# Splitting a third chunk of the mixer's output product, and issuing gate and spill loads from POOL's queue

## The chip, the cores and the metric

The kernel runs on one core of a Trainium2 chip. TensorE (PE) does the matrix products; VectorE (DVE), ScalarE (ACT) and GpSimd (POOL) do the elementwise work; SyncE (SP) only issues DMA transfers, and ACT and POOL can issue them too. Sixteen DMA engines move the data. The metric is the device time of one execution in microseconds: before the change 3697.25 us, the median of three runs (3697.02 to 3698.64).

## The reference

Two blocks of two layers each on tokens of width 1024. The first block takes 256 tokens `x` and 256 context tokens `ctx`. A layer mixes tokens (differential attention, a pooling branch and a convolution branch, gated and summed) and then applies a PEER network: per token and head the 16 best of 128 x 128 experts are chosen, and their rows of `u` and `v` used.

```python
# mixer, layer l: h is x (256 tokens), hc is ctx (256 tokens)
merged = g[:, :, 0] * attn + g[:, :, 1] * pool + g[:, :, 2] * conv
mix = merged @ w_out                       # 1024 x 1024
h = h + mod[:, 2] * mix                    # ctx alike, with its own mod
xn2 = modulate(rms_norm(h, norm2_g[l]), mod[:, 3], mod[:, 4])
# PEER: eidx and gate come from the top 16 of q @ sub_keys
hid = gelu(einsum('td,thkd->thk', xn2, u_emb[eidx]))
h = h + mod[:, 5] * einsum('thk,thkd->td', gate * hid, v_emb[eidx])
```

The second layer needs `ctx` only for keys and values. The second block (retention and block-sparse attention) is not touched by the change.

## The kernel before, in words

**Products.** Activations lie transposed, with the width on the partitions in eight chunks of 128 and the tokens along the free axis. A product in float32 is made of three matmuls of reduced precision: each operand is split into a high and a low half, and hi·hi, lo·hi and hi·lo are accumulated (lines 393 to 395; one output chunk of 128 takes 8 x 3 matmuls). A weight unit of 1 MB is loaded by SP into a buffer `wraw` (`wload`, line 348, its DMA in line 351). ACT writes the high half (`uhi` or `vhi`, line 361), DVE the low half (`ulo` or `vlo`, line 362). The buffer is free for the next load when DVE has read it. In the values loop these buffers form a ring of three.

**The mixer's output product** (`mixer_out`, line 1022). In layer 0 x and ctx are multiplied by `w_out` together, 512 columns at a time. Chunks below `whole` (line 1061) are done that way; the others are done for x first, then for ctx, 256 columns each. After a chunk, DVE adds it to the residual (`hT`, line 1088), ACT squares it, and POOL and DVE add up the squares (`ssacc`, line 445). When x's chunks are complete, `norm_split` takes the mean of the squares on PE (`ps_ss`, line 464), the inverse root on POOL (`rst`, line 470), spreads it with PE (`ps_y`), and DVE and ACT make the normed halves `xl` and `xh` (lines 491 to 496), while PE does ctx's chunks. Then the same for ctx, and PE can start the PEER queries.

**PEER, layer 0.** 384 of 512 tokens are handled densely: all 16384 experts are evaluated, and a gate tensor with zeros for the experts that weren't chosen is multiplied in. The experts come in 64 blocks of 256. While the gates are being found, the hidden values of the first 42 blocks are computed ahead and written to DRAM (`hd`); the expanded gates are in DRAM too (`gd`). The last 128 ctx tokens are handled by rows: POOL gathers the chosen rows of `u` and then of `v` with 128 + 128 indirect DMAs (class `Rows`, line 258, one row per token and gather, 512 KB). They go into five buffers, and each gather waits for a marked matmul of PE ("beat"), so that they are spread over PE's work. DVE multiplies and sums a `u` row (line 274), PE sums the `v` rows (`ps_row`, line 307).

**The values loop** goes over the 64 blocks. For each, `prep` (line 1199) fetches the gates `G` (line 1556, 768 KB for two blocks, two buffers), gets the hidden values, multiplies both on DVE (line 1213) and splits the result into `Wh` (ACT, line 422) and `Wl` (DVE, line 423). For the 42 blocks computed ahead the hidden values are loaded back (`hs_r`, line 1209, 384 KB, two buffers); for the other 22 they are computed on the spot, in `hidden` with `ps_mm`. Blocks of both kinds alternate in pairs, and the last 20 blocks are all of the first kind. PE then adds the block's product with `v` into PSUM: four accumulators `keep` for 256 tokens, and two `ps_v` that DVE adds to `racc` (line 1236). `values_tok` (line 1269) holds the matmuls. In the same stretch the next layer's modulation weights `wraw_m` are loaded (line 624).

SP's list before holds the loads of weights, `G` and `hs_r` in the order in which the program asks for them, POOL's list the row gathers. The very first `G` is issued by POOL. In layer 1 there are no rows, and `self.rows` is None.

Of the kernel before, what the change touches and what calls it, by code (L numbers as in the profile page):

```python
# [23 lines left out]
KD = 8  # L24
# [305 lines left out]
class Prog:  # L330
# [689 lines left out]
    def mixer_out(self, l, merged, hT, T, right, bulk):  # L1020

        nc, w = self.nc, self.g[f"wa{l}"]
        segs = [(s * 256, (s + 1) * 256) for s in range(T // 256)]
        sts = [self.sumsq(256) for _ in segs]

        def add(c, ps, n, t0, t1):
            self.residual(l, 2, c, hT, ps, t0, t1, old)
            for i, (a, b) in enumerate(segs):
                if t0 <= a and b <= t1:
                    self.sumsq_add(sts[i], hT[:, c, a:b], c)  # L1030
        with ExitStack() as cx:
            mp = cx.enter_context(self.tc.tile_pool(name=f"mp4{l}", bufs=1, reuse_waits="tile"))
            self.pn = cx.enter_context(self.tc.tile_pool(name=f"pn{l}", bufs=1, space=PSUM, reuse_waits="tile"))
            mh = mp.tile([P, KD, T], F32R, tag="mh", name="mh")
            ml = mp.tile([P, KD, T], F32R, tag="ml", name="ml")
            old = hT
            if l == 0:
                old = mp.tile([P, KD, 512], F32, tag="old", name="old")
            k = 0
            for _ in chain([0], bulk):  # L1040
                while k < 6 and k in self.pooled:
                    self.split(mh[:, k], ml[:, k], merged[:, k])
                    k += 1
            ple = None
            if l == DEPTH - 1:
                ple = self.ple(0, lambda tt, h: hT[:, 4 * tt + 2 * h:4 * tt + 2 * h + 2, 0:256], mp)
                next(ple)
            it = self.units(f"wa{l}", 45, 4)
            units = [next(it) for _ in range(3)]
            for k in range(0, KD if l == 0 else 0, 2):  # L1050
                nc.sync.dma_start(old[:, k:k + 2], self.g["hx"][:, k:k + 2])
            first = self.chunks_mm(units, mh, ml, 0, T, range(KPOOL[l]))
            self.pool_out(l, self.last_pool, T, (self.pn, "py", 2))
            self.chunks_mm(units, mh, ml, 0, T, range(KPOOL[l], 6), first, KPOOL[l])
            for k in range(6, KD):
                self.split(mh[:, k], ml[:, k], merged[:, k])
            self.chunks_mm(units, mh, ml, 0, T, range(6, KD), first, 6)
            right.close()
            if l == 0:
                hT = self.resid()  # L1060
            whole = KD if T == 256 else 6
            for c in range(whole):
                add(c, first.pop(0)[:, :T] if first else self.chunk_mm(next(it), mh, ml, 0, T), 0, 0, T)
                if c == 5 and l == DEPTH - 1:
                    self.turn_residual(hT, 0)
            ends = [next(it) for _ in range(whole, KD)]
            xn = None
            for i, (t0, t1) in enumerate(segs):
                for c, unit in zip(range(whole, KD), ends):
                    add(c, self.chunk_mm(unit, mh, ml, t0, t1), i, t0, t1)  # L1070
                if i == 0:
                    self.preload(f"wa{l}", range(49, 51 - l))
                if ple:
                    next(ple)
                xn = self.norm_split(hT, sts[i], lambda k, s: self.mod[:, l, 4, k, s:s + 1],
                                     lambda k, s: self.mod[:, l, 3, k, s:s + 1], [(i, t0, t1)], out=xn, first=t0, mid=ple)
            self.dump(f"h{l}m", hT)
            if l == DEPTH - 1:
                self.turn_residual(hT, 1)
                for _ in ple:  # L1080
                    pass
        return xn, hT
# [117 lines left out]
    def prep(self, l, b, xh, xl, T, gd, hd):  # L1200

        nc = self.nc
        G = self.gates(l, b, gd, T // GSTAGE, T)
        hs = self.hsp.tile([P, 2, T], F32, tag="hs", name="hs_r", bufs=2)
        if b >= NLEAD[l]:
            for _ in self.hidden(l, b, xh, xl, T, hs):
                pass
        else:
            nc.sync.dma_start(hs, hd[b])
        Wh = self.pp.tile([P, 2, T], F32R, tag="Wh", name="Wh", bufs=2)  # L1210
        Wl = self.pp.tile([P, 2, T], F32R, tag="Wl", name="Wl", bufs=2)
        w = hs.rearrange("p j (q t) -> p j q t", t=GSTAGE)
        nc.vector.tensor_tensor(w, w, G.rearrange("p q j t -> p j q t"), op=ALU.mult)  # L1213
        self.split(Wh, Wl, hs)
        return Wh, Wl
# [334 lines left out]
    def gates(self, l, b, gd, nq, T):  # L1550
        nc = self.nc
        key = (l, b // 2)
        if self.gcur is None or self.gcur[0] != key:
            G = self.pp.tile([P, nq, 4, GSTAGE], F32, tag="G", name="G", bufs=2)
            n = nq if self.gcur else nq - 1
            (nc.sync if self.gcur else nc.gpsimd).dma_start(G[:, :n].rearrange("p q j t -> p q (j t)"),
                              gd[:n, :, (b // 2) * 4:(b // 2) * 4 + 4, :].rearrange("q p j t -> p q (j t)"))
            if n < nq:
                nc.gpsimd.tensor_copy(G[:, n], self.glast)
            self.gcur = (key, G)  # L1560
        return self.gcur[1][:, :, (b % 2) * 2:(b % 2) * 2 + 2, :]
# [367 lines left out]
```

## Time and profile before

| | |
|---|---|
| time, median of 3 runs | 3697.25 us (3697.02 to 3698.64) |
| profiled execution | 3701.45 us, span 3699.7 us |
| PE busy | 3574.0 us, 97% of the span |
| DVE, ACT, POOL busy | 67%, 44%, 16% |
| DMA traffic | 777.60 MB, mean 210 GB/s |
| of it queue q1, in hardware | 567.29 MB |
| of it queue q0, in software (POOL's) | 135.41 MB |

Busy time is counted per engine; an engine that isn't busy either waits for another or has nothing to do. A row of waits names the engine that waited, and after the arrow what ended its wait. In the timeline a figure in brackets is the idle time just before the instruction. A DMA's row on SP or POOL is its issue, and not the transfer.

### The profile page before, as it was taken

How to read it: one execution, taken by the hardware profiler on the slowest of the kernel's cores; microseconds unless marked ns; L12 is line 12 of the kernel's file. 1: busy time of each engine (PE TensorE's matmuls, PEld its weight loads, DVE VectorE, ACT ScalarE, POOL GpSimd, SP SyncE). 2: the span in 40 equal slices, each digit the busy share in tenths (PEclk: the TensorE clock that was granted, in tenths of full speed). 3: DMA queues.
4: the chain of work that ended last, by engine and by line, in shares of the span. 5: the costliest groups of instructions: out<-in, count | busy, mean ns of one | idle time of the engine just before them, and what ended most of it. 6: DMA issues, size and time to landing. Idle time of an engine off the chain costs nothing.

```text
span 3699.7 us, 55016 instructions
## 1 busy us (share of the span) xinstructions
PE 3574.0 (97%) x21681; PEld 3097.0 (84%) x21681; DVE 2461.5 (67%) x4540; ACT 1634.3 (44%) x2608; POOL 604.0 (16%) x686
## 2 busy tenths in 40 slices
PE   7999999899999998999999999999999999999999
PEld 5988877789999877776766799999998888887787
DVE  5566556599697777744445677778876555557675
ACT  3334333336576322222222354555676444445454
POOL 0112222100011232322222121221000000002121
PEclk9999999999999999999999999999999999999999
DMA  5222145224689898888889533354578766766453
GB/s 212 75 86 80 69 154 216 75 83 170 228 323 336 315 332 306 325 295 309 298 321 325 188 115 120 120 175 160 200 269 292 244 236 237 242 231 212 145 174 111
DMA packets 227763, 777.60 MB, mean 210 GB/s; under 512 B 17296, under 2 KB 100752, under 8 KB 168496
## 3 DMA queue, kind: packets, MB, share of 16 engines
q1 hardware_dynamic: 165984, 567.29, 43.7%
q0 software_dynamic: 37184, 135.41, 10.4%
q10 hardware_dynamic: 24336, 71.38, 5.0%
q8 instruction: 170, 2.79, 0.3%
q14 instruction: 89, 0.73, 0.1%
HBM read 705.60 MB, written 68.42 MB: 209 GB/s over the span
## 4 chain that ended last, share of the span: by engine, by line
PE 41%; DVE 4%; DMA 2%; ACT 1%; issue 1%; POOL 1%; DVEq 0%; ACTq 0%; SPq 0%; POOLq 0%
PE keep L1269 12%; PE ps_mm L393 5%; PE ps_mm L395 5%; PE ps_mm L394 5%; PE ps_wide L395 2%; PE ps_wide L393 2%; PE ps_wide L394 2%; PE ps_v L1269 1%; DVE ulo L362 1%; PE ps_nar L393 1%; PE ps_nar L395 1%; PE ps_nar L394 1%; DMA wraw<-in_v 1%; PE ps_mm L414 1%; PE ps_row L307 1%
## 5 line engine op out<-in xcount | busy, mean ns | idle before, releaser
L361 ACT ACTIVATE uhi<-wraw 128x1024 fp32r<-128x1024 f32 x586 | 609.0, 1057 | 879.2 <-PE ps_mm L394 336.1
L393 PE MATMUL ps_mm<-xh,uhi 128*128 128x256 f32 (+2 forms) x2952 | 955.5, 324 | 9.2 <-ACT hs L1566 3.7
L395 PE MATMUL ps_mm<-xh,ulo 128*128 128x256 f32 (+2 forms) x2952 | 940.8, 319 | 7.1 <-DVE ulo L362 7.1
L362 DVE TENSOR_TENSOR ulo<-wraw,uhi 128x1024 fp32r<-128x1024 f32 x586 | 718.0, 1237 | 340.6 <-ACT uhi L361 317.6
L394 PE MATMUL ps_mm<-xl,uhi 128*128 128x256 f32 (+2 forms) x2952 | 939.9, 318 | 0.0
L393 PEld LDWEIGHTS ps_mm<-xh,uhi 128*128 128x128 f32 x2952 | 562.5, 191 | 54.0 <-issue 9.2
L395 PEld LDWEIGHTS ps_mm<-xh,ulo 128*128 128x128 f32 x2952 | 562.2, 191 | 29.4 <-DVE ulo L362 8.0
L394 PEld LDWEIGHTS ps_mm<-xl,uhi 128*128 128x128 f32 x2952 | 562.7, 191 | 20.8
L362 DVE TENSOR_TENSOR vlo<-wraw,vhi 128x1024 fp32r<-128x1024 f32 x184 | 224.0, 1222 | 187.7 <-ACT vhi L361 187.5
L361 ACT ACTIVATE vhi<-wraw 128x1024 fp32r<-128x1024 f32 x184 | 193.2, 1056 | 338.1 <-DMA wraw<-in_v 176.0
L1269 PE MATMUL keep<-vlo,Wh 128*128 128x512 f32 x656 | 256.7, 391 | 3.6 <-DVE vlo L362 3.6
L1269 PE MATMUL keep<-vhi,Wh 128*128 128x512 f32 x656 | 257.8, 393 | 0.5 <-ACT Wh L422 0.5
L1269 PE MATMUL keep<-vhi,Wl 128*128 128x512 f32 x656 | 256.2, 391 | 0.3 <-DVE Wl L423 0.3
L258 POOL DMA_INDIRECT row<-in_urow,eu x128 | 158.5, 1238 | 589.7 <-PE ps_mm L395 440.7
L1213 DVE TENSOR_TENSOR hs_r<-hs_r,G 128x768 f32<-128x768 f32 (+1 forms) x128 | 105.2, 823 | 170.7 <-DMA hs_r<-hd 106.9
L393 PE MATMUL ps_nar<-uhi,xh 128*128 128x256 f32 x704 | 201.3, 286 | 2.3 <-ACT cs L664 2.3
L394 PE MATMUL ps_nar<-ulo,xh 128*128 128x256 f32 x704 | 200.1, 284 | 0.0
L395 PE MATMUL ps_nar<-uhi,xl 128*128 128x256 f32 x704 | 199.9, 284 | 0.0
L258 POOL DMA_INDIRECT row<-in_vrow,ev x128 | 136.0, 1063 | 375.4 <-PE keep L1269 180.2
L1530 ACT ACTIVATE stage<-ps_g 128x512 f32<-128x512 f32 x160 | 165.1, 1160 | 1.7 <-DMA wraw<-in_u 0.8
L274 DVE CUSTOM_DVE_ANT_0 row<-row,xt 128x1024 f32<-128x1024 f32 x128 | 155.2, 1219 | 4.5 <-DMA row<-in_urow,eu 4.5
L1269 PEld LDWEIGHTS keep<-vhi,Wh 128*128 128x128 f32 x656 | 123.7, 189 | 36.8 <-issue 9.2
(428 smaller groups left out, 6965.2 us busy)
## 6 DMA issues: line engine op xcount, KB each, us to landing
wraw<-in_u SPq DMA_DIRECT2D x128, 1024.0 KB
wraw<-in_v SPq DMA_DIRECT2D x128, 1024.0 KB
wraw<-in_wa SPq DMA_DIRECT2D x104, 1024.0 KB
wraw<-in_wb SPq DMA_DIRECT2D x50, 1024.0 KB
gd<-stage ACTq DMA_DIRECT2D x80, 512.0 KB
wraw_m<-in_wmod SPq DMA_DIRECT2D x24, 1024.0 KB
G<-gd SPq DMA_DIRECT2D x31, 768.0 KB
mraw<-in_wmod SPq DMA_DIRECT2D x16, 1024.0 KB
```

The lines of the kernel that those rows point to most:

```text
L258: ins = self.nc.gpsimd.indirect_dma_start(row, None, self.p.g[name], bass.IndirectOffsetOnAxis(ap=idx, axis=0))
L274: ins = nc.vector.tensor_tensor_reduce(out=row, in0=row, in1=self.xt, op0=ALU.mult, op1=ALU.add, scale=1.0, scalar=0.0, accum_out=self.hid ...
L307: nc.tensor.matmul(ps[c:c + 32, :], m[:, g, :], rows[n - 4 + g][:, h * 512:(h + 1) * 512], start=(i == 0), stop=(i == 31), tile_position=( ...
L361: nc.scalar.activation(hi, r, AF.Copy)
L362: nc.vector.tensor_tensor(lo, r, hi.bitcast(F32), op=ALU.subtract)
L393: nc.tensor.matmul(ps, lh, rh, start=(i == 0), stop=False)
L394: nc.tensor.matmul(ps, lh, rl, start=False, stop=False)
L395: self.beat = nc.tensor.matmul(ps, ll, rh, start=False, stop=(i == n - 1))
L414: self.nc.tensor.matmul(ps[:, t0:t1], a[:, s], b[:, k, t0:t1], start=(n == 0 and i == 0), stop=(n == KD - 1 and i == 2))
L1213: nc.vector.tensor_tensor(w, w, G.rearrange("p q j t -> p j q t"), op=ALU.mult)
L1269: self.beat = self.nc.tensor.matmul(ps, a[:, j, t], b[:, c], start=(start and j == 0 and i == 0), stop=(stop and j == 1 and i == 2), skip_ ...
L1530: nc.scalar.activation(st[:, :, tb:tb + 4].rearrange("p j t -> p t j"), pg, AF.Copy, scale=1.0 / GSCALE)
```

## The change

In line 1061 `whole` becomes 5 for layer 0, so chunks 5, 6 and 7 of the output product are computed for x and ctx apart; before, these were 6 and 7. In lines 1209 and 1556 the loads of `hs_r` and `G` are issued by POOL instead of SP as long as `self.rows` is set, which is in layer 0.

```diff
@@ mixer_out
-            whole = KD if T == 256 else 6
+            whole = KD if T == 256 else 5
@@ prep
-            nc.sync.dma_start(hs, hd[b])
+            (nc.gpsimd if self.rows else nc.sync).dma_start(hs, hd[b])
@@ gates
-            (nc.sync if self.gcur else nc.gpsimd).dma_start(G[:, :n]...)
+            (nc.sync if self.gcur and not self.rows else nc.gpsimd).dma_start(G[:, :n]...)
```

On POOL, at the start of layer 0's values loop, the row gathers stood in two unbroken runs; the difference shows what stands among them now (`row<-in_urow` is a gather, x9 means nine in a row):

```order
-L258 DMA row<-in_urow,eu 128x1024 x96
-L258 DMA row<-in_vrow,ev 128x1024 x128
+L1556 DMA G<-gd_6364 128x12x128
+L258 DMA row<-in_urow,eu 128x1024 x9
+L1209 DMA hs_r<-hd_6365 128x768
+L258 DMA row<-in_urow,eu 128x1024 x2
+L1556 DMA G<-gd_6364 128x12x128
+L258 DMA row<-in_urow,eu 128x1024
+L1209 DMA hs_r<-hd_6365 128x768
+L258 DMA row<-in_urow,eu 128x1024 x2
+L1556 DMA G<-gd_6364 128x12x128
+L258 DMA row<-in_urow,eu 128x1024 x11
```

Each load now stands between gathers, two loads of each kind for every pair of blocks computed ahead in the first part of the loop.

On SP, in the same place, the loads that stood between weights are gone (`wraw_m` are modulation weights):

```order
 L351 DMA wraw<-in_u 128x2048
-L1209 DMA hs_r<-hd_6340 128x768
-L624 DMA wraw_m<-in_wmod 128x2048
-L1209 DMA hs_r<-hd_6340 128x768
-L1556 DMA G<-gd_6339 128x12x128 x2
-L351 DMA wraw<-in_v 128x2048
-L351 DMA wraw<-in_u 128x2048
-L351 DMA wraw<-in_v 128x2048
-L624 DMA wraw_m<-in_wmod 128x2048
-L351 DMA wraw<-in_v 128x2048 x2
-L1209 DMA hs_r<-hd_6340 128x768
-L351 DMA wraw<-in_u 128x2048
```

The weights follow in the order they had, with nothing between them.

On DVE, in the mixer's output product of layer 0, the residual additions `hT` of ctx stand behind x's norm (`n`, `xl`):

```order
+L362 TENSOR_TENSOR ulo<-wraw,uhi 128x1024
+L496 SCALAR_TENSOR_TENSOR xl<-n_6221,mod,xh 128x256
 L496 SCALAR_TENSOR_TENSOR xl<-n_6225,mod,xh 128x256
 L496 SCALAR_TENSOR_TENSOR xl<-n_6229,mod,xh 128x256
-L496 SCALAR_TENSOR_TENSOR xl<-n_6233,mod,xh 128x256
-L1088 SCALAR_TENSOR_TENSOR hT<-ps_mm,mod,old 128x256 x2
+L1088 SCALAR_TENSOR_TENSOR hT<-ps_mm,mod,old 128x256 x3
 L218 CAST idr<-ident 128x128
 L445 TENSOR_TENSOR ssacc<-ssacc,sq 128x256
 L466 TENSOR_SCALAR rst<-ps_ss 128x2
```

Three additions follow where two did, and three splits of a weight's low half stand among the norm's instructions instead of two.

## Rows read from the trace of the kernel before

**Rows 1.** The page, its first part: busy time, share of the span and instructions of each engine.
```profile
PE 3574.0 (97%) x21681; PEld 3097.0 (84%) x21681; DVE 2461.5 (67%) x4540; ACT 1634.3 (44%) x2608; POOL 604.0 (16%) x686
```
**Rows 2.** Windows of the values loop: length, busy us, then granted clock, DMA share, GB/s.
```profile
1190.00:1600.00 410.00, 380.35 (x1817) 322.60 (x1816) 290.33 (x393) 122.28 (x150) 127.09 (x104) 0.96 0.87 317
1600.00:2100.00 500.00, 490.81 (x2417) 343.14 (x2416) 239.12 (x328) 131.71 (x153) 131.77 (x126) 0.99 0.86 305
```
**Rows 3.** PE's waits from 1190 to 1600 us: total, times, longest.
```profile
PE ps_mm L393 <- DVE racc L1236: 16.1, 6, 4.5
PE ps_mm L393 <- ACT uhi L361: 7.3, 2, 4.2
```
**Rows 4.** Timeline from 1310 us: start, duration, engine, line, instruction.
```profile
1310.56 0.33 SPq L1209 DMA_DIRECT2D hs_r<-hd  x1
1310.93 7.06 SPq L1556 DMA_DIRECT2D G<-gd  x2
...
1317.52 1.22 DVE L362 TENSOR_TENSOR ulo<-wraw,uhi 128x1024 fp32r<-128x1024 f32 x1
...
1318.76 0.35 SPq L351 DMA_DIRECT2D wraw<-in_v  x1
```
**Rows 5.** Timeline from 1328 us, the end of the same chain.
```profile
1328.13 2.00 ACT L361 ACTIVATE uhi<-wraw 128x1024 fp32r<-128x1024 f32 x2 [7.51 <-DMA wraw<-in_v]
...
1332.64 0.68 DVE L1236 TENSOR_TENSOR racc<-racc,ps_v 128x512 f32<-128x512 f32 x1
...
1333.38 0.45 PE L393 MATMUL ps_mm<-xh,vhi 128*128 128x384 f32 x1 [3.91 <-DVE racc L1236]
```
**Rows 6.** Windows of PE's wait and of what follows it, columns as above.
```profile
1329.40:1333.30 3.90, 0.07 (x1) 0.00 (x0) 3.90 (x6) 0.73 (x1) 1.51 (x1) 1.00 1.01 417
1333.30:1336.80 3.50, 3.42 (x14) 3.42 (x15) 1.78 (x5) 1.10 (x2) 0.00 (x0) 0.70 1.03 419
```
**Rows 7.** Windows behind the mixer, columns as above.
```profile
699.70:713.30 13.60, 10.88 (x45) 10.01 (x46) 6.64 (x17) 5.51 (x13) 0.71 (x1) 0.50 0.20 72
713.30:720.00 6.70, 6.70 (x57) 6.70 (x56) 0.00 (x0) 0.00 (x0) 0.00 (x0) 0.98 0.01 2
```
**Rows 8.** Timeline of the mixer's end, 690 to 700 us.
```profile
693.29 1.22 DVE L362 TENSOR_TENSOR ulo<-wraw,uhi 128x1024 fp32r<-128x1024 f32 x1
...
697.19 0.87 DVE L1088 SCALAR_TENSOR_TENSOR hT<-ps_mm,mod,old 128x256 f32<-128x256 f32 x2
...
698.34 0.72 POOL L445 TENSOR_TENSOR ssacc<-ssacc,sq 128x256 f32<-128x256 f32 x1 [10.58 <-ACT sq L434]
...
699.67 0.56 PE L464 MATMUL ps_ss<-mean,ssacc 128*128 128x1 f32 x2 [7.47 <-DVE ssacc L445]
```
**Rows 9.** DMA from 1190 to 2100 us: queue q0, and issues with KB each.
```profile
q0 software_dynamic: 32736, 119.22, 36.8%
...
G<-gd SPq DMA_DIRECT2D x31, 768.0 KB
...
hs_r<-hd SPq DMA_DIRECT2D x42, 384.0 KB
```
**Rows 10.** The tile G: engine, operation, count, ns minimum, median and maximum, first and last.
```profile
L1556 POOL DMA_DIRECT2D G<-gd x2: 1067/1122/1176, 1190.3 to 2828.5; - x2
```
**Rows 11.** Waits of all engines from 1190 to 2100 us.
```profile
POOL row L258 <- PE keep L1269: 227.5, 86, 10.6
...
DVE row L274 <- DMA row<-in_urow,eu: 4.5, 3, 2.4
```
**Rows 12.** Windows with POOL's G in flight, then SP's, columns as above.
```profile
1192.00:1196.00 4.00, 4.00 (x25) 4.00 (x24) 2.26 (x2) 1.44 (x2) 0.00 (x0) 1.00 1.03 418
1201.00:1204.00 3.00, 3.00 (x20) 3.00 (x19) 0.00 (x0) 0.86 (x1) 0.94 (x1) 1.00 1.05 339
```
**Rows 13.** SP's waits from 1190 to 2100 us.
```profile
SPq L1556 <- DVE hs_r L1213: 120.0, 20, 8.9
SPq L1209 <- DVE Wl L423: 112.7, 26, 10.1
```
**Rows 14.** The line of the row gathers, 1190 to 2100 us, columns as for the tile G.
```profile
L258 POOL DMA_INDIRECT row<-in_vrow,ev x128: 934/937/1966, 1586.7 to 2079.5; - x128
```

More of the change, by code (lines that the diff above doesn't have):

```diff
@@ L1555, in gates @@
             n = nq if self.gcur else nq - 1
-            (nc.sync if self.gcur else nc.gpsimd).dma_start(G[:, :n].rearrange("p q j t -> p q (j t)"),
+            (nc.sync if self.gcur and not self.rows else nc.gpsimd).dma_start(G[:, :n].rearrange("p q j t -> p q (j t)"),
                               gd[:n, :, (b // 2) * 4:(b // 2) * 4 + 4, :].rearrange("q p j t -> p q (j t)"))
```

## The prediction

> **What bounds the kernel now.** Of the page I read the engine row first [rows 1]: TensorE (PE) is busy 97% of the span, so only its remaining idle time and its stretches at the low clock can be won. The profiled execution took 3701.45 us (span 3699.7, 1.75 around it), 4.20 above the median of 3697.25; I work out differences in it and take them from the median. Two places are touched: the norm behind the mixer's output product (about 690 to 720 us), and layer 0's values loop (1190 to 2100 us), the only place where `self.rows` is set.
>
> Next come the windows of the values loop [rows 2]. The first 410 us hold 29.65 us without a matmul, the other 500 hold 9.19. The mean granted clock of the first stretch is 0.96. The DMA engines are busy 87 and 86% of the two, so weights, gates and spilled hidden values arrive with little to spare.
>
> PE's own table of waits in the first stretch [rows 3] gives 16.1 us, in six waits, to VectorE's (DVE) `racc` and 7.3, in two, to ScalarE's (ACT) `uhi`: 23.4 of the 29.65. These are links of one chain, which the timeline shows in full [rows 4, 5]. SyncE (SP) issues an hs, two G loads until 1317.99, and at 1318.76 the weight load `wraw<-in_v`. ACT waits for that load until 1328.13, 9.4 us after its issue; DVE splits the low halves behind ACT, a row reduction and the `racc` follow, which frees a PSUM buffer, and PE starts at 1333.38 after 3.91 us idle. The wait put down to DVE is thus a late weight. The windows around it [rows 6] show two more things: while PE waits, the DMA engines run full (share 1.01, 417 GB/s), and behind the wait the granted clock is 0.70, so part of these 3.5 us ran at the lower of the two levels.
>
> **The change part by part.**
>
> *Mixer.* Chunk 5 is computed as two products of 256 columns instead of one of 512: 24 matmuls of 512 columns go, 48 of 256 come. The columns in all are the same, so I leave PE's own time unchanged. A matmul of 256 columns takes 6.70/57 = 0.1175 us [rows 7]. The x half is now followed by three ctx products of 24 x 0.1175 = 2.8 us each instead of two, so x's norm may start 2.8 us earlier against the end. On DVE x's norm ran up to the `hT` pair at 697.19, where the ctx residuals went on, and PE stood idle until 699.67 for the sum of their squares [rows 8]. Of the 2.8 us, one more `ulo` inside the norm takes 1.2, a third `hT` 0.4, a second POOL addition of squares 0.7 (each from its row there [rows 8]). That leaves 2.8 - 1.2 - 0.4 - 0.7 = 0.5 gained. Bounds: if the shorter gap let PE keep its clock, the 10.88 busy us at 0.50 behind it [rows 7] would take 5.4 less; if nothing starts earlier, 1.2 + 0.4 + 0.7 = 2.3 are lost. I take 0.5, since PE still stands idle some 7 us before.
>
> *Issue.* SP loses 31 G and 42 hs issues, POOL gains them. An hs took SP 0.33 us [rows 4, 9]; SP does nothing but issue, so this bounds nothing. On POOL two G loads took 1.12 us in the middle [rows 10]; 73 x 1.12 = 82 us are added. POOL was busy 127.09 and 131.77 of these 910 us [rows 2] and its row gathers wait mostly for PE's beat [rows 11]; the other 651 us hide the 82. Without that cover each of the rows behind a load would start 1.1 us late.
>
> *Queue.* A transfer on SP's queue stands behind what SP issued before it. In the chain shown the weight stood behind an hs and two Gs. A G of 768 KB takes 2.5 us at 317 GB/s [rows 2], an hs of 384 KB 1.2: 3.7 for one of each, which no longer lie in front of the weights. But the bytes don't go away, and the engines are nearly full. From both sides: nothing is gained where G takes its share beside the weight as it took it before it; 23.4 us where both kinds of wait go. I take half of the 3.7 for each of the six places at which PE stood idle for `racc`: 6 x 1.85 = 11.1 us. Behind a shorter stall the clock returns sooner: a mean of 0.96 over 410 us costs at most 0.04 x 410 = 16 us; I take 2, since most stalls only shorten. The second stretch has little to give, and I count nothing there.
>
> *Form of the transfer.* A G from SP's queue, moving nearly alone, showed 339 GB/s at share 1.05; with the G of POOL's queue among the transfers it was 418 at 1.03 [rows 12]. 31 x 0.79 MB = 24.4 MB cost 72 us at the first rate, 58 at the second: 14 us of DMA time less in the whole loop. It is why I take half of 3.7 and not less; it is not added again.
>
> *What is added.* On POOL the loads wait for buffers as they did on SP: a G for the product L1213 that reads its buffer, an hs for the `Wl` two jobs back. SP stood 120.0 us in 20 such waits and 112.7 in 26, the longest 8.9 and 10.1 [rows 13]. Behind them now stand row gathers, and behind a late row DVE's L274, or for v rows PE itself. A row has room: 128 v rows from 1586.7 to 2079.5 [rows 14] are one per 3.9 us, and a row is used three gathers or more after its own issue, some 12 us. Also, q0 moved 119.22 MB [rows 9] and is given 24.4 + 16.5 (42 hs) = 41 more. Today L274 waits for a row three times, 4.5 us in all, 1.5 each [rows 11]. I take three more such waits, of which PE feels less than half: +2. Bounds: 0, and one such wait for each of the 31 pairs of loads, +46.
>
> The Trainium skill has a rule against this change: "DMA: Bandwidth & Descriptors", section "Issuing engines are not separate DMA queues", says that transfers from all issuing engines interleave on the same 16 DMA engines, and that a further issuing engine saves only issue time. By it the 11.1 and the 2 of the clock would be nothing, and rival 3 comes out. The full engines at the stall [rows 6] agree with it; no run before the change shows the G loads on another queue.
>
> **Sum.** -0.5 (mixer) - 11.1 (queue) - 2 (clock) + 2 (rows) = -11.6: 3697.25 - 11.6 = 3685.65, say 3685.7. Its own range is 3674 (all of 3.7 us in each of six places, 22.2 for 11.1) to 3693 (a third of it, 3.7).
>
> **The rivals.**
>
> 1. *Late rows, slower.* In the lead-only end of the loop a load stands on POOL between every two or three rows, and each waits for its buffer. A row gathered behind a wait of 10 us has used up most of its 12; then PE waits for `ps_row`, DVE for L274. For it: SP's 232.7 us of waits for these buffers [rows 13]. Against: POOL waited 227.5 us for `keep` alone [rows 11], and buffer and beat waits overlap. If each of 31 pairs costs PE half a late row, 0.75 us, that is +23; less the 13.6 gained, +9.6 or 3707. It decides from 13.6/31 = 0.44 us per pair on.
>
> 2. *All stalls go.* If the weights come in time everywhere, 23.4 us go and half of the clock's 16: 31 less, 3666. For it: the load in the chain shown follows close behind a G. Against: the full DMA engines, and the buffer: DVE's `ulo` ran until 1318.74, SP issued at 1318.76 [rows 4]. That load waited for the buffer, not for the issue of G.
>
> 3. *Hidden anyway.* Weights are issued when a buffer comes free and land when the bytes are through, and neither changes. Only the mixer's 0.5 and a stall's worth of better order remain, about -1: 3696. For it the same 1318.76, and the share of 1.01; against it the 14 us of DMA time that go.
>
> **How the numbers follow.** Chances: forecast 0.52, late rows 0.19, all stalls gone 0.07, hidden 0.22. A measurement of this kernel tells about 0.2%, 7.4 us, from no change: 3689.9 and 3704.6 are the bounds. The upper end of the forecast's range lies past the first, so 0.46 of its 0.52 is faster, with rival 2 that is 0.53; 0.06 and rival 3 make 0.28 the same; rival 1 is slower, 0.19. The range takes in rival 3 whole, rival 1 somewhat past its middle and rival 2's near half: 3665 to 3711.
>
> **What would show it.** In the profile after, SP should issue weights alone in this loop, and q0 carry some 160 MB. The forecast is right if PE's waits for `racc` and `uhi` in the first stretch fall from 23.4 us to about 12, its clock there rises above 0.96, and L274's wait for rows stays under 10 us. Rival 1 comes true if PE's `ps_row` or L274 wait tens of us for rows, above all after 1870. In the mixer, PE's idle time before the ctx `ps_ss` should stay between 6 and 8 us. The forecast is wrong as a whole if the 29.65 idle us stay and the time doesn't change: then the queue in which G lies was never what delayed the weights.

## The result, and the profile after the change

The changed kernel takes 3751.52 us (median of 4 runs, 3747.47 to 3760.32) against 3697.94 for the kernel before (median of 4, the three runs of above among them): a ratio of 1.0146, 95% interval 1.0125 to 1.0166, or 54 us slower. The forecast was 3685.7, and the range ended at 3711. The profiled execution of the kernel after took 3760.32 us (span 3758.5), so differences between profiles are some 5 us larger than those between medians.

Its page has the engines' busy time and the queues' traffic over the whole span (before: [rows 1] and the table of the profile before):

```profile
PE 3590.5 (96%) x21705; PEld 3101.1 (83%) x21705; DVE 2460.5 (65%) x4540; ACT 1635.4 (44%) x2608; POOL 672.1 (18%) x759
...
q1 hardware_dynamic: 111824, 526.39, 39.8%
q0 software_dynamic: 46992, 176.31, 13.7%
```

41 MB went from q1 to q0 as announced. POOL is busy 68 us more, 58 of them with issuing the 73 loads (31 x 1.07 and 42 x 0.6 us, shown further down). The windows of the values loop, which now ends some 60 us later [rows 2]; columns are length, busy us of PE, its weight loads, DVE, ACT and POOL, then granted clock, DMA share and GB/s:

```profile
1190.00:1600.00 410.00, 366.72 (x1746) 312.58 (x1745) 281.67 (x381) 117.05 (x144) 150.03 (x124) 0.95 0.85 307
1600.00:2160.00 560.00, 525.49 (x2494) 360.78 (x2493) 246.33 (x341) 137.85 (x161) 178.38 (x178) 0.96 0.79 280
```

Before, 4234 matmuls began here in 910 us; now 4240 in 970. PE's idle time went from 38.84 to 77.79 us, and the same matmuls were busy 892.21 us instead of 871.16, since the granted clock fell from 0.99 to 0.96 in the second stretch. So 39 us are waits, and 21 us are matmuls that ran longer at a lower mean clock. The DMA engines are less busy than before in the second stretch, 79% for 86%: the same bytes take longer, although on average the engines had time left.

The waits in the loop [rows 3, 11] tell which came new. Two of before that stand in no row above:

```profile
DVE hs_r L1213 <- DMA hs_r<-hd: 84.3, 23, 7.2
...
PE ps_row L307 <- DMA row<-in_vrow,ev: 0.9, 2, 0.6
```

After:

```profile
DVE hs_r L1213 <- DMA hs_r<-hd: 158.9, 32, 11.0
...
PE ps_row L307 <- DMA row<-in_vrow,ev: 29.6, 8, 9.8
PE ps_mm L393 <- DVE racc L1236: 24.7, 8, 8.7
...
PE ps_mm L393 <- ACT uhi L361: 11.3, 2, 5.7
...
DVE row L274 <- DMA row<-in_urow,eu: 4.1, 2, 2.3
```

In the first stretch alone the line for `racc` is

```profile
PE ps_mm L393 <- DVE racc L1236: 21.0, 6, 8.7
```

and that for `uhi` the same 11.3. So these two, 23.4 us before in this stretch, didn't fall to 12 us but rose to 32.3. PE now waits for gathered `v` rows, and DVE nearly twice as long for the hidden values that are loaded back, while L274's wait for `u` rows stayed as it was. The timeline shows one of PE's waits for a `v` row from its start, with the issues on POOL:

```profile
1922.05 0.58 POOL L1209 DMA_DIRECT2D hs_r<-hd  x1 [10.52 <-DVE Wl L423]
...
1922.93 0.96 POOL L258 DMA_INDIRECT row<-in_vrow,ev  x1 [0.30 <-PE ps_v L1269]
...
1927.92 1.07 POOL L1556 DMA_DIRECT2D G<-gd  x1 [4.03 <-DVE ulo L362]
...
1929.30 0.97 POOL L258 DMA_INDIRECT row<-in_vrow,ev  x1 [0.30 <-issue]
...
1930.57 1.45 POOL L258 DMA_INDIRECT row<-in_vrow,ev  x1 [0.30 <-issue]
...
1932.37 0.59 POOL L1209 DMA_DIRECT2D hs_r<-hd  x1 [0.35 <-DVE Wl L423]
...
1933.26 0.96 POOL L258 DMA_INDIRECT row<-in_vrow,ev  x1 [0.30 <-issue]
...
1934.53 0.93 POOL L258 DMA_INDIRECT row<-in_vrow,ev  x1 [0.30 <-issue]
...
1942.20 1.93 PE L307 MATMUL ps_row<-row,mask 128*32 128x512 f32 x6 [9.77 <-DMA row<-in_vrow,ev]
```

POOL stood 10.5 us for the buffer of an hs load, then two hs, a G and five rows went into the same queue within 13 us, and PE stood 9.8 us for one of these rows. It looks like rival 1, word for word. The experiments show that such waits, by themselves, cost next to nothing.

In the mixer PE's wait for the squares of ctx is 6.6 us instead of 7.5 [rows 8]:

```profile
700.56 0.99 PE L464 MATMUL ps_ss<-mean,ssacc 128*128 128x1 f32 x4 [6.62 <-DVE ssacc L445]
```

### The profile page after: what moved, and what is told of

Its sections match the earlier page's. It is cut to its first block, busy times and chain, and to the rows that moved or that the text cites. A ratio compares the mean times of both kernels' runs of the same rounds, so it can differ in the third digit from the quotient of the medians.

```text
span 3758.5 us, 55071 instructions
## 1 busy us (share of the span) xinstructions
PE 3590.5 (96%) x21705; PEld 3101.1 (83%) x21705; DVE 2460.5 (65%) x4540; ACT 1635.4 (44%) x2608; POOL 672.1 (18%) x759
## 2 busy tenths in 40 slices
DMA packets 183411, 777.60 MB, mean 207 GB/s; under 512 B 17296, under 2 KB 53136, under 8 KB 124144
## 4 chain that ended last, share of the span: by engine, by line
PE 75%; DMA 9%; DVE 8%; issue 3%; ACT 3%; POOL 2%; ACTq 0%; SPq 0%; DVEq 0%; POOLq 0%
PE keep L1269 13%; PE ps_mm L393 12%; PE ps_mm L394 12%; PE ps_mm L395 12%; DMA wraw<-in_v 3%; DMA hs_r<-hd 3%; PE ps_v L1269 3%; PE ps_nar L393 2%; PE ps_nar L395 2%; PE ps_nar L394 2%; PE ps_wide L395 2%; PE ps_wide L394 2%; PE ps_wide L393 2%; PE ps_mm L414 2%; DVE ulo L362 2%
## 5 line engine op out<-in xcount | busy, mean ns | idle before, releaser
L395 PEld LDWEIGHTS ps_mm<-xh,ulo 128*128 128x128 f32 x2952 | 562.4, 191 | 29.6 <-DVE ulo L362 7.9
L422 ACT ACTIVATE Wh<-hs_r 128x768 fp32r<-128x768 f32 (+1 forms) x128 | 93.1, 728 | 156.6 <-DVE hs_r L1213 99.7
L274 DVE CUSTOM_DVE_ANT_0 row<-row,xt 128x1024 f32<-128x1024 f32 x128 | 155.4, 1220 | 4.1 <-DMA row<-in_urow,eu 4.1
```

Of the source, the lines that this page charges most:

```text
L274: ins = nc.vector.tensor_tensor_reduce(out=row, in0=row, in1=self.xt, op0=ALU.mult, op1=ALU.add, scale=1.0, scalar=0.0, accum_out=self.hid ...
L395: self.beat = nc.tensor.matmul(ps, ll, rh, start=False, stop=(i == n - 1))
L422: nc.scalar.activation(hi, src, AF.Copy)
```

## The experiments

All are edits of the kernel before, except where the changed kernel is named. Ratios are to the kernel before in the same session, with 95% intervals.

**The parts one by one (e1 to e4, and e15).**

```diff
e1, e15: whole = ... 5 alone       e2: hs on nc.gpsimd alone       e3: G on nc.gpsimd alone
e4: both on nc.gpsimd if self.rows and not 22 <= b < 42    (not in the end of 20 loaded blocks)
```

> Only the split of the third chunk; all loads stay on SP. Both theories put the loss of 54 us into the values loop, so both expect 3697 +- 3 us here. If the split itself were the cause, the time would be 3745 or more.

> Of the change only the hs loads on POOL's queue (42 loads, 16.5 MB); G on SP, mixer as before. Theory A (a load that waits on POOL for its buffer keeps the row gathers behind it, and PE waits for the rows; SP's waits for hs buffers were 113 us): most of the loss, 3725 to 3755. Theory B (all that goes through q0 gets slower, by the bytes put there): 16.5 of 41 MB, so 22 of 54 us, 3719. Theory C (G is the load that blocks): about 3697.

> Of the change only the G loads on POOL's queue (31 loads, 24.4 MB); hs on SP, mixer as before. Theory A with hs as the blocking load: 3690 to 3712. Theory B: 24.4 of 41 MB, 32 of 54 us, 3730. Theory C: 3735 or more, with waits of POOL for the product that reads G.

> Both loads on POOL as in the change, but only in the part of the loop in which blocks computed on the spot alternate with blocks loaded back (G of the 44 blocks there, hs of 22); in the end of 20 loaded blocks both stay on SP; mixer as before. Theory A: the loss falls to that of the first part, 3697 to 3715, and PE's wait for v rows goes away for the most part. Theory B: the bytes there are 26 of 41 MB, so 34 of 54 us, 3731.

Measured: e1 0.9992 (0.9981 to 1.0003), e2 1.0037 (1.0023 to 1.0052), e3 1.0038 (1.0023 to 1.0052), e4 1.0080 (1.0063 to 1.0097). The mixer isn't the cause. The loads are, but not one of them: hs alone costs 14 us, G alone 14, both together 54. No theory had both right: by the bytes (theory B) hs would have cost 22 us and G 32, by POOL's waits for hs (theory A) hs alone 28 or more. And e4 loses 30 us in the part where theory A expected at most 18 and theory B 34.

> The split of the third chunk alone once more, with more rounds: 3693 to 3697, ratio 0.9990 to 0.9998 as far as e1 (0.9992) told; the sum of the prediction has 0.5 us for it.

Measured: 0.9993 (0.9984 to 1.0003), as in e1. Both point to 2 to 3 us gained, neither is clear of nothing.

**POOL's waits without the bytes (e5, e7 and e6).** In e5 the order on POOL is nearly that of the change, POOL waits for the same buffers, and the bytes stay on SP's queue.

```diff
 e5, ahead of each load on SP:
+            if self.rows:
+                nc.gpsimd.memset(hs[:, 0, 0:1], 0.0)      # G alike
             nc.sync.dma_start(hs, hd[b])
 e7, in the load's place; self.preps holds each block's product and Wl:
+            tk = nc.gpsimd.memset(self.rows.tok, 0.0)     # waits for Wl of preps[m - 2], the product of preps[m - 3]
 e6: the memset of tok as in e7 without a wait, and the load on SP waits for it
```

> The kernel before, with both loads on SP; but ahead of each such load POOL writes one column of the load's buffer in its own list. So POOL waits for the buffer as in the change, and the load waits for POOL, while the bytes stay on SP's queue. Theory A (the order on POOL costs the time: rows behind a waiting load, or loads behind rows that wait for PE's beat): 3735 to 3755. Theory B (the transfers in q0 cost it): 3697 to 3703.

> The kernel before; in the place of each load POOL waits for the DVE instruction that frees the load's buffer (the Wl two jobs back for hs, the product two pairs back for G), while the load itself stays on SP and waits for nothing more. Theory A1: 3730 to 3755, PE's wait for v rows tens of us. Theory A2 and theory B: 3697 to 3703.

> The kernel before; each load on SP waits for a mark that POOL sets in its list behind the row gathers ahead of it. POOL waits for no buffer, so rows are never late for a load. Theory A1 (rows stand behind loads): 3697 to 3703. Theory A2 (loads stand behind rows that wait for PE's beat, so they are fetched late): 3730 to 3755, with DVE's wait for hs well above 84 us. Theory B: 3697.

Measured: e5 1.0014 (1.0004 to 1.0023), e7 0.9999 (0.9985 to 1.0013), e6 1.0008 (0.9997 to 1.0018). e6 tells nothing of the order on POOL: with nothing to wait for, its 73 marks were set at 700 to 712 us, long before the loop. The other two tell much. POOL's waits for buffers in the changed kernel, then in e5, then in e7:

```profile
POOL G L1556 <- DVE hs_r L1213: 87.1, 21, 8.2
...
POOL hs_r L1209 <- DVE Wl L423: 51.0, 13, 13.4
```
```profile
POOL G L1559 <- DVE hs_r L1215: 58.5, 19, 8.1
POOL hs_r L1210 <- DVE Wl L423: 47.1, 16, 9.3
```
```profile
POOL tok L1209 <- DVE Wl L425: 62.2, 28, 8.7
POOL tok L1565 <- DVE hs_r L1219: 33.9, 10, 6.1
```

By these rows POOL stands 106 us in e5 and 96 us in e7 in front of waiting rows, and the kernel is 5 us slower in the one and no slower in the other. Rows behind a wait of up to 9 us come in time. So theory A alone falls, and with it the mechanism of rival 1, as far as these waits go; those of the changed kernel are longer, 138 us, one of them 13.4. Run e14, below, has as many as the changed kernel.

**Issue, bytes and weights (e9, e14, e10).** e9 and e14 split each load: POOL issues a part, SP the rest, at the same places.

```diff
 e9: z = 32 of 384 columns of hs, 1 of 12 slices of G;  e14: z = half of both
+            nc.gpsimd.dma_start(hs[:, :, :z], hd[b][:, :, :z])
+            nc.sync.dma_start(hs[:, :, z:], hd[b][:, :, z:])
 e10: the changed kernel; SP's next weight load waits for a memset that POOL does behind each G or hs load
```

> Each load split: POOL issues a twelfth of it from its own queue (one 128-token-group slice of G, the first 32 of 384 columns of hs), SP the rest; so POOL waits for the same buffers at the same places, and spends the issue of a software DMA each time, but q0 gets 3.4 MB instead of 41. Theory B (bytes in the rows' own queue): 3697 to 3705, q0 at some 123 MB in the loop. Theory D (POOL's time to issue 73 more DMAs, 1.1 and 0.6 us each): 3730 or more.

> As e9, but POOL issues half of each load and SP the other half; 20 MB more in q0, mixer as before. If the cost grows with the bytes, between e9 (3709) and the changed kernel (3752): 3720 to 3738. If what is left over e9 sets in only when a whole load is in the rows' queue: under 3715.

> The changed kernel with both loads on POOL; but the next weight load on SP waits for POOL's mark behind each G or hs load, so the weights can't run ahead of G and hs as they could not before. Theory B: as the changed kernel, 3740 to 3755 or more. Theory E (on a list of its own SP sends weights sooner, and they take the DMA engines from G, hs and rows): 3697 to 3715.

Measured: e9 1.0030 (1.0020 to 1.0041), e14 1.0072 (1.0057 to 1.0088), e10 1.0157 (1.0139 to 1.0175). Weights that run ahead are not it: e10, where they can't, is as slow as the change. With the same places and the same count of software issues the cost rises with the part of the bytes that goes into the rows' queue: 11 us with a twelfth, 27 with half, 54 with all (some 57 without the 2 to 3 that the mixer's split seems to give). POOL's waits for buffers in e14 are those of the changed kernel:

```profile
POOL G L1561 <- DVE hs_r L1216: 87.4, 19, 8.7
...
POOL hs_r L1211 <- DVE Wl L423: 50.1, 16, 7.9
```

So is the time that POOL spends on issues. The issues of G and of hs, in e14 and then in the changed kernel:

```profile
L1561 POOL DMA_DIRECT2D G<-gd x33: 872/882/1171, 1190.4 to 2855.9; - x33
```
```profile
L1211 POOL DMA_DIRECT2D hs_r<-hd x42: 734/751/778, 1239.2 to 2109.6; - x42
```
```profile
L1556 POOL DMA_DIRECT2D G<-gd x33: 1060/1073/1171, 1190.6 to 2886.0; - x33
```
```profile
L1209 POOL DMA_DIRECT2D hs_r<-hd x42: 576/602/622, 1243.1 to 2138.5; - x42
```

For 31 G and 42 hs that is 59 us with half a load and 58 with a whole one. From e14 to the changed kernel waits and issue time on POOL stay as they are, the bytes in its queue double, and the cost doubles; besides, SP then issues no part of the loads, and the mixer's split comes in. What e9 has over e5, 6 us with intervals that overlap, is POOL's issues, a second DMA for each load and the first 3.4 MB; theory B had e9 at 3705 at most.

**Order within the queue (e12, e13).** In the changed kernel the scheduler had put loads ahead of older gathers. e12 holds each load behind the gathers that the program asks for first; e13 has the same order on POOL with the bytes on SP.

```diff
 e12, the changed kernel, G alike; self.rows.got is the latest gather:
+            add_manual_dep(ld.ins, self.rows.got.ins.name, NoSync)      # order on POOL only
 e13: as e5, with the same line for the memset
```

> The changed kernel, with each load of G and hs held behind the row gathers that the program asks for before it (in the changed kernel the scheduler had put loads up to five gathers ahead of older ones). The bytes in the rows' queue are the same 41 MB, but POOL should hardly wait for buffers any more, and no older row stands behind a load. Theory B alone (bytes in the queue): still 3735 to 3755. Theory A with B (POOL's waits bunch loads and rows, and in one queue the rows of a bunch come after the loads): 3697 to 3712. Loads that come too late instead: 3715 to 3735, with DVE's wait for hs above the 159 us of the changed kernel.

> The order of e12 on POOL, with the loads on SP: in each load's place POOL writes one column of the load's buffer, behind the same row gathers as in e12, and SP's load waits for it. If the place in the list is what made the loads of e12 late: 3735 to 3750, with PE's wait for Wh some 60 us. If it is the queue they share with the rows: 3697 to 3712, and PE's wait for Wh under 15 us.

Measured: e12 1.0121 (1.0104 to 1.0138), e13 1.0057 (1.0042 to 1.0072). PE's waits in e12, then in e13:

```profile
PE keep L1272 <- ACT Wh L423: 66.8, 16, 7.7
...
PE ps_row L308 <- DMA row<-in_vrow,ev: 0.3, 1, 0.3
```
```profile
PE keep L1273 <- ACT Wh L423: 40.2, 12, 8.2
...
PE ps_row L308 <- DMA row<-in_vrow,ev: 1.3, 2, 0.8
```

In e12 POOL waits for no load's buffer and rows are on time, but now `Wh` is late, since hs and G are. DVE's wait for hs is 174.6 us. The answer lies between the two that e13 was to tell apart: 21 of the 45 us are the later place in POOL's list; the other 24, a difference between two sessions, go with issuing the loads on POOL and sending them through its queue. The landing times show part of what the queue does. From issue to landing, median, in the last stretch (1885 to 2100 us), in e5 (loads in a queue apart), the changed kernel (loads ahead of rows) and e12 (rows ahead of loads):

```profile
hs_r<-hd SPq DMA_DIRECT2D x19, 384.0 KB, 5.9
G<-gd SPq DMA_DIRECT2D x8, 768.0 KB, 7.6
...
row<-in_vrow,ev POOLq DMA_INDIRECT x50, 7.5
```
```profile
hs_r<-hd POOLq DMA_DIRECT2D x18, 384.0 KB, 6.7
G<-gd POOLq DMA_DIRECT2D x9, 768.0 KB, 6.4
...
row<-in_vrow,ev POOLq DMA_INDIRECT x48, 9.1
```
```profile
G<-gd POOLq DMA_DIRECT2D x9, 768.0 KB, 10.6
hs_r<-hd POOLq DMA_DIRECT2D x18, 384.0 KB, 10.5
...
row<-in_vrow,ev POOLq DMA_INDIRECT x47, 7.9
```

In this stretch, what stands behind in the shared queue lands late: rows 1.6 us later than apart in the changed kernel, hs 4.6 and G 3.0 us later in e12. In e6, which also has the loads in a queue apart, rows took 7.2, hs 5.2 and G 8.0 us, so two such runs differ by less. The section "Two DMAs through the same engine are not ordered" of the Trainium skill's page "DMA: Bandwidth & Descriptors" says that in one queue of a DMA engine descriptors start in order, which agrees with the times of this stretch.

Ahead of it the landing times show nothing of the kind. From 1600 to 1880 us, in e5 and in the changed kernel:

```profile
hs_r<-hd SPq DMA_DIRECT2D x11, 384.0 KB, 6.0
row<-in_vrow,ev POOLq DMA_INDIRECT x73, 6.9
```
```profile
hs_r<-hd POOLq DMA_DIRECT2D x8, 384.0 KB, 7.2
row<-in_vrow,ev POOLq DMA_INDIRECT x69, 6.6
```

e6 has 7.8 and 6.3 there. Yet e4, in which only this earlier part has its loads on POOL, loses 30 us. How the shared queue costs time there stays open.

**A third queue (e11), and one more chunk (e8).**

```diff
 e11: nc.scalar in the place of nc.gpsimd for both loads of the changed kernel;   e8: whole = ... 4, loads on SP
```

> The changed kernel, with the loads of G and hs on ACT's queue instead of POOL's: off SP's queue, and not in the rows' queue either. Theory B: the rows are on time, no more than 5 us of waits of PE for v rows; ACT stands in front of waiting loads now and then, 3690 to 3715. Theory E: 3740 or more, since the weights run ahead here too.

> The kernel before with four of eight chunks split (whole = 4), loads on SP. With three the loop began 2.3 us earlier than before in its profile; x's norm again starts 2.8 us earlier against the end, one more ulo, hT and square addition again take some of it: 3690 to 3697. If the square additions on POOL have become the end of the chain, no gain over three.

Measured: e11 1.0067 (1.0042 to 1.0091), e8 1.0003 (0.9993 to 1.0012). On ACT's queue the rows are on time (PE waits 1.5 us for them, once), and half of the loss is gone; what is left, 25 us, is more than theory B had (3715) and isn't taken apart here: ACT's own work may now stand behind loads that wait for buffers, and the loads have left SP's queue here too. So weights alone on SP's queue bring no gain here either. A fourth split chunk gives nothing over the kernel before.

## Why the prediction was wrong

*What is added* is the step that failed. It took three more late rows at L274, +2 us, and weighed only POOL's waits for buffers. These it read rightly, and alone they cost next to nothing (e5 and e7: 5 and 0 us); L274's wait for rows didn't grow at all (4.1 us for 4.5). What it passed over in one sentence, that q0 moved 119 MB already and is given 41 more, is the cost: some 43 of the 54 us (the changed kernel less e9), and in the profile it stands in PE's wait for `v` rows, 29.6 us for 0.9, in DVE's for hs, and in matmuls at a lower clock. The bound of +46 was made of the wrong thing, and was too low.

*Queue* failed next. There was no 11.1 us to gain. The prediction's own evidence against it was right: SP's load at 1318.76 was issued when DVE had freed its buffer [rows 4], so G's issue in front of it delayed nothing. And weights land no sooner when they are alone on SP's queue. From issue to landing, median, 1200 to 1590 us, in e5 (G and hs on SP) and in the changed kernel:

```profile
wraw<-in_v SPq DMA_DIRECT2D x26, 1024.0 KB, 7.2
wraw<-in_u SPq DMA_DIRECT2D x15, 1024.0 KB, 8.0
```
```profile
wraw<-in_v SPq DMA_DIRECT2D x23, 1024.0 KB, 7.9
wraw<-in_u SPq DMA_DIRECT2D x14, 1024.0 KB, 8.9
```

e6, with G and hs on SP too, has 7.5 and 8.9. PE's waits for `racc` and `uhi` in the first stretch are 32.3 us, more than the 23.4 of before [rows 3]. On ACT's queue (e11) the wait for `racc` there is 16.1 us, as before; that of `ps_mm` for `uhi` fell to 0.8, but `keep` waits 10.9 us for `uhi` and `ulo` where it waited 4.0. With the 11.1 the 2 us for the clock fall: [rows 6] has the low clock right behind a wait, the waits grew, and the same matmuls took 21 us longer.

*Issue*, counted at nothing, costs a few us at most: e9 over e5, 6 us for the issues, the second DMA of each load and 3.4 MB together. The issues took POOL 58 us and not 82, since an hs takes 0.6 us and not 1.12.

*Form of the transfer* was right as to the form: the page after counts 53136 packets under 2 KB for 100752. But the 14 us of DMA time that were to go did not. In the loop the packets of q0 and q1 took 36.8 and 48.5% of 910 us before, and 48.2 and 32.3% of 970 us after: 776 and 781 us. The busy share of the engines fell only because the loop got longer.

*Mixer*: 0.5 us was forecast, e1 and e15 have 2 to 3 us with intervals that take in no change and the 0.5. PE's wait shortened by 0.85 us.

*Rival 1* had the right side and the right sign in the profile, PE's `ps_row` waiting for rows, 23.1 of its 29.6 us after 1870, at 3707; the measured loss is more than five times its 9.6 us. Its mechanism, the 10 us waits that use up a row's 12 us, isn't borne out by e5 and e7: without the bytes the waits cost 5 us and nothing. That its sign came is in part luck. *Rival 3* had the reason why nothing was to be gained. The rule of the Trainium skill that stands beside it in the prediction (page "DMA: Bandwidth & Descriptors", section "Issuing engines are not separate DMA queues"), that another issuing engine saves issue time only, gives 3696; the measurement has 3751.5 and decides. The rule speaks of the engines that all queues share; here it made a difference which queue the loads went into.

Open: why the cost doesn't go by the bytes alone. G alone (24 MB) costs 14 us and hs alone (16.5 MB) 14, but half of both (20 MB) 27 and all of both 54. A queue close to its limit would behave so, and so would two loads that come in one bunch; no run tells these apart. Nor does one tell how much is the order inside POOL's queue and how much comes with taking the loads off SP's: e11, with nothing added to the rows' queue, still loses 25 us.

No version tried beats the kernel before clearly. The nearest is the mixer's split alone: 3693.65 against 3695.29 us, with an interval that takes in no change.

## What to carry to other kernels

Before moving a load to another engine's queue, list what already goes through that queue, with its bytes and how urgent it is; the engine's idle time says nothing on that. A wait in an issuing list that looks like the cause can be tested by leaving the wait and taking the bytes away, which costs one line. And where a queue's order is suspected of a delay, look first at what released the load: if it was a buffer, the issues in front did not hold it. Whether the bytes in front did is seen in its landing time, with them and without.

## What the runs showed of the hardware

With DMA engines 85 and 79% busy in the two stretches of the loop, moving 41 of its 283 MB from SP's queue into POOL's cost 1.5%; half of these bytes, with the same waits and issue time on POOL, cost 0.7%. The two orders in one queue came out at nearly the same total (1.0146 and 1.0121) with quite different waits, and in the last stretch the landing times differ with them: 9.1 us for the rows in the one, 10.5 for hs in the other. And 96 us of waiting on POOL, in front of gathers that feed PE, cost nothing that could be measured.
